# RWKV's triangular solve in blocks of 16 instead of 32, and every weight tile's low part on VectorE

## The chip, the cores and the metric

The kernel runs on one core of one Trainium2 chip, as one program. The metric is the device time of one launch in microseconds (us), the median of several runs. Five engines work side by side, each through its own instructions in order: TensorE (PE: matmuls, and PEld: its weight loads), VectorE (DVE), ScalarE (ACT), GpSimd (POOL) and SyncE (SP), which issues all DMAs of this kernel.

## The reference

One transformer-like block over 1024 positions of width 1024, in float32. A normalised input goes through one projection (`w_in`, 1024 x 3200), whose columns feed four mixers of 256 channels each: chunked attention, HGRN2, RWKV-7 and RG-LRU. Their outputs are joined, projected by `w_out`, normalised and added to the input; an MLP with squared ReLU (1024 to 4096 to 1024) follows.

```python
proj = (rms_norm(x, g_pre) @ w_in)
ya, yb, yc, yd = chunk_attention(..), hgrn2(..), rwkv7(..), rglru(..)
x = x + rms_norm(concatenate([ya, yb, yc, yd]) @ w_out, g_post)
x = x + rms_norm(square(relu(rms_norm(x, g_mlp) @ w1)) @ w2, g_mlp_post)
```

What matters here is RWKV-7's step, a recurrence over time with a state per head:

```python
sa = einsum('bhvk,bhk->bhv', state, -kk)
state = state * w + sa[..., None] * (kk * a) + v[..., None] * k
```

In chunks of 64 steps, the dependence of `sa` on earlier `sa` of the same chunk is a unit lower-triangular 64 x 64 system for each chunk and head. Its inverse is needed for 8 chunks and 4 heads, 32 systems, in each half of the sequence.

## The kernel before

The sequence is done in two halves of 512 positions (`hf` 0 and 1). For each half the four mixers run in the order of `ORDER`: RWKV, attention, LRU, HGRN in the first, RWKV, HGRN, attention, LRU in the second. Their instructions interleave: a planner orders each engine's instructions by a modelled time and by priorities (`PRIO`, `at(...)`), so the text's order is not the order on the engines. After that comes the output projection (`out_load`, `out_mm`, `residual`), and from about 715 us on the MLP, a Strassen-like scheme.

Matmuls are done in three passes for precision. A weight tile of 128 x 1024 is loaded raw (`wr`, L167), rounded by ScalarE to a high part (`wh`, L176), and the difference is the low part (`wl`, L178). With `hi` and `lo` of the activations, PE does `wh*hi`, `wl*hi` and `wh*lo` (L318 to L320, L345 to L347, L1023 to L1025). Raw, high and low tiles have two buffers each. `wparts` makes `wl` on GpSimd unless it is given an engine. Of 66 tiles 57 are made on GpSimd; the first tile of all and the eight of the second half's output projection on VectorE.

RWKV inverts each 64 x 64 system in `rwkv`, section `Ri`. The 64 x 64 matrix is cut into blocks of 32. `Ld` holds the diagonal blocks, `Lo` the block below. `Ld` goes through DRAM (`d1`) into `Lb`, with one system's rows in one partition: 64 blocks, each twice, since the two halves of the partitions do 16 columns of the inverse each. A loop of 31 steps on VectorE, two instructions each (L501 a product into `tmpx`, L503 a sum into `X`), is the substitution. `X` and its transpose go to DRAM (`d2`, L508, L509), and come back as matrices by partition in `XT` and `X11` (L516, L518). Two matmul stages of 64 small products (`p1`, L525; `p2`, L536) join the two 32-blocks to the 64 x 64 inverse in `XT`, which the recurrence over chunks (`Rk`) uses.

HGRN builds its attention in six levels: GpSimd makes `z` (L735, L736), ScalarE its exponential (L737), VectorE `z` and `zq` (L738, L747), PE `pz` (L750), VectorE writes it into `att` (L752). The names that the rows show besides: `pdg` (L264) spreads a column over rows at the start; `lx` (L931) is LRU's input; `q` (L698, L839) are HGRN's and attention's queries; `gg` and `th` (L719, L715) are HGRN's gate.

Of the kernel before, what the change touches and what calls it, by code (L numbers as in the profile page):

```python
# [20 lines left out]
F32 = mybir.dt.float32  # L21
# [6 lines left out]
MULT, ADD, SUB, MAX, MIN = ALU.mult, ALU.add, ALU.subtract, ALU.max, ALU.min  # L28
# [3 lines left out]
P = 128  # L32
# [8 lines left out]
CH = 64  # L41
# [47 lines left out]
def body(ctx: ExitStack, tc: tile.TileContext, A: dict, out: bass.AP, dbg=None, stop_after=None):  # L89
    nc = tc.nc  # L90
    V, S, G, T = nc.vector, nc.scalar, nc.gpsimd, nc.tensor

    const = ctx.enter_context(tc.tile_pool(name="const", bufs=1))
    dram = ctx.enter_context(tc.tile_pool(name="dram", bufs=1, space=DRAM))
# [6 lines left out]
    def at(*key):  # L101

        sec.close()
        n = PRIO.get("".join(map(str, key)), 0)
        if n:
            sec.enter_context(tc.high_priority(offset=n))

    def nm(base):
        uid[0] += 1
        return f"{base}_{uid[0]}"  # L110

    def bank(name, tag="pa"):
        return psp.tile([P, 512], F32, tag=tag, name=nm(name), bufs=PB[tag])
# [56 lines left out]
    def wload(src, eng=None):  # L170
        return wparts(wraw(src), eng)

    def wparts(raw, eng=None):
        wp = wpool[0]
        hi = wp.tile([P, 1024], F32R, tag="wh", name=nm("wh"))
        S.copy(hi[:], raw[:])  # L176
        lo = wp.tile([P, 1024], F32R, tag="wl", name=nm("wl"))
        (eng or G).tensor_tensor(lo[:], raw[:], hi[:].bitcast(F32), SUB)  # L178
        return hi, lo

    def split(eng_lo, hi, lo, src, scale=None):
# [15 lines left out]
    def u(name, dt=F32):  # L197
        return ma.tile([P, 512], dt, tag="ua", name=nm(name), bufs=NA)

    def u3(name, w, dt=F32):  # L200
        return ma.tile([P, 512 // w, w], dt, tag="ua", name=nm(name), bufs=NA)
# [13 lines left out]
    def w4(name, shape):  # L215
        return mx.tile(shape, F32, tag="w4", name=nm(name), bufs=2)
# [51 lines left out]
    def prep0():  # L268
        nc.sync.dma_start(vecs[:], A["vecs"])
        cols = W_LO, W_K  # L270
        hs, xs, ws = [], [], []
        for k in range(NK):
            xs.append(xload(0, k, lambda s, d, name: hp.tile(s, d, tag="hl", name=name, bufs=NLO)))
            if k < 2:
                ws.append(wraw(wsrc[cols[k]][0]))
        nc.sync.dma_start(ident[:], A["ident"])
        for k, h in enumerate(xs):
            hs.append(parts_in(0, k, h))
            if k < 2:
                early[cols[k]] = wparts(ws[k], (V, G)[k])  # L280
        stats(0)
        proj_pair(hs, *cols)
        spread(0)
        return hs
# [37 lines left out]
    def proj_fm(hs, col):  # L322

        if col in done:
            return done.pop(col)
        wh, wl = wload(wsrc[col][0])
        ps = bank("fm", "fm")
        for k in range(NK):
            mm_in(ps, wh, wl, hs, k)
        return ps  # L330
# [25 lines left out]
    def rwkv_shift(hf, ps, j, name):  # L356

        om = consts["om"]
        pc = u("pcs")
        V.tensor_tensor(pc[:], ps[:], rb_[hf][:], MULT)  # L360
        tmp = u("shtmp")
        S.activation(tmp[:], pc[:], AF.Identity, scale=om[:, j:j + 1])
        xs = u(name)
        V.scalar_tensor_tensor(xs[:, 1:TH], pc[:, 0:TH - 1], vec("mu", j), tmp[:, 1:TH], MULT, ADD)
        if hf == 0:
            V.tensor_copy(xs[:, 0:1], tmp[:, 0:1])
            V.tensor_copy(lastc[:, j:j + 1], pc[:, TH - 1:TH])
        else:
            V.scalar_tensor_tensor(xs[:, 0:1], lastc[:, j:j + 1], vec("mu", j), tmp[:, 0:1], MULT, ADD)
        return xs  # L370

    def rwkv(hf, hs):
# [13 lines left out]
        for j in range(2):  # L386
# [16 lines left out]
            k = rwkv_shift(hf, proj_fm(hs, W_K + j * P), 2 + j, "xk")  # L403
# [12 lines left out]
            for t in range(4):  # L416
                T.matmul(pss[:, 2 * t:2 * t + 2], sq[:, t * P:(t + 1) * P], consts["bones"][:],
                         start=True, stop=True)
# [15 lines left out]
            r = rwkv_shift(hf, proj_fm(hs, W_R + j * P), j, "xr")  # L434
# [30 lines left out]
        Ld, Lo = u3("Ld", 32), u3("Lo", 32)  # L465
# [8 lines left out]
        for b in range(4):  # L474
            r = slice(32 * b, 32 * b + 32)
            cc = 32 * (b % 2)
            S.copy(Ld[r].rearrange("q (p n) t -> q p n t", p=2), p4[r, :, :, cc:cc + 32])
        for c in range(2):
            r = slice(64 * c, 64 * c + 32)
            S.copy(Lo[r].rearrange("q (p n) t -> q p n t", p=2), p4[r, :, :, 32:64])  # L480
        at("Ri", hf)


        d1 = dram.tile([64, 32, 32], F32, tag="d1", name=nm("d1"), bufs=2)
        d2 = dram.tile([2, 64, 32, 32], F32, tag="d2", name=nm("d2"), bufs=2)
        d1v = d1[:].rearrange("(n b) s t -> b s n t", b=4)
        for b in range(4):
            nc.sync.dma_start(d1v[b], Ld[32 * b:32 * b + 32, :, :])
        Lb = w4("Lb", [P, 32, 32])
        for q in range(2):  # L490
            nc.sync.dma_start(Lb[64 * q:64 * q + 64], d1[:])
        X = u3("X", 16)
        G.memset(X[:], 0.0)
        for q in range(2):
            xq = X[64 * q:64 * q + 64, 16 * q:16 * q + 16, :].rearrange("p r c -> p (r c)")
            G.memset(xq[:, 0:256:17], 1.0)
        tmpx = u("tmpx")
        for jj in range(31):
            nr, ncl = 31 - jj, min(jj + 1, 16)
            tv = tmpx[:, 0:nr * ncl].rearrange("p (r c) -> p r c", c=ncl)  # L500
            V.tensor_tensor(tv, Lb[:, jj, jj + 1:32].unsqueeze(2).to_broadcast([P, nr, ncl]),  # L501
                            X[:, jj, 0:ncl].unsqueeze(1).to_broadcast([P, nr, ncl]), MULT)
            V.tensor_tensor(X[:, jj + 1:32, 0:ncl], X[:, jj + 1:32, 0:ncl], tv, ADD)  # L503
        XTt = u3("XTt", 32)
        V.tensor_copy(XTt[:], X[:].rearrange("p r c -> p c r"))
        for q in range(2):
            pq = slice(64 * q, 64 * q + 64)
            nc.sync.dma_start(d2[0, :, :, 16 * q:16 * q + 16], X[pq])  # L508
            nc.sync.dma_start(d2[1, :, 16 * q:16 * q + 16, :], XTt[pq])  # L509
        XT = w4("XT", [P, 16, CH])  # L510
        X11 = u3("X11", 32)
        d2v = d2[:].rearrange("k (n b) s t -> k b s n t", b=4)
        for b in range(4):
            r = slice(32 * b, 32 * b + 32)
            cc = 32 * (b % 2)
            nc.sync.dma_start(XT[r, :, cc:cc + 32], d2v[1, b])  # L516
            if b % 2 == 0:
                nc.sync.dma_start(X11[r, :, :], d2v[0, b])  # L518
            else:
                G.memset(XT[r, :, 0:32], 0.0)  # L520
        p1 = bank("p1")
        p13 = p1[:].rearrange("p (n c) -> p n c", c=32)
        for n in range(16):
            for c in range(2):
                T.matmul(p13[64 * c + 32:64 * c + 64, n, :], Lo[64 * c:64 * c + 32, n, :],  # L525
                         X11[64 * c:64 * c + 32, n, :], start=True, stop=True)
        T1 = u3("T1", 32)
        for c in range(2):
            r = slice(64 * c + 32, 64 * c + 64)
# [3 lines left out]
        for n in range(16):  # L533
            for c in range(2):
                r = slice(64 * c + 32, 64 * c + 64)
                T.matmul(p23[64 * c:64 * c + 32, n, :], T1[r, n, :], XT[r, n, 32:64], start=True, stop=True)  # L536
        for c in range(2):
            r = slice(64 * c, 64 * c + 32)
            S.copy(XT[r, :, 32:64], p23[r])

# [4 lines left out]
        for uu in range(2):  # L545
            for i in range(2):
# [28 lines left out]
                for o, M in ((pr, L2), (py, Ak)):  # L575
                    for h in range(4):
                        j, p = h // 2, h % 2
                        for cc in range(2):
                            T.matmul(o[half(cc), half(h)], M[p][j][half(cc)], vt[j][half(cc), ti, half(p)],
                                     start=(h == 0), stop=False, skip_group_check=True)  # L580
                for cc in range(2):
                    c = 2 * ti + cc
                    r = slice(64 * cc, 64 * cc + 64)
# [12 lines left out]
                    for h in range(4):  # L596
                        j, p = h // 2, h % 2
                        n = 8 * p + 2 * ti + j
                        T.matmul(pu[r, 64 * h:64 * h + 64], XT[r, n, :], Rs[r, 64 * h:64 * h + 64],
                                 start=False, stop=True, skip_group_check=True)  # L600
                    S.copy(Us[r, :], pu[r, :])
                    psS = bank("psS")
                    for h in range(4):
                        j, p = h // 2, h % 2
                        o = psS[64 * p:64 * p + 64, j * CH:(j + 1) * CH]
                        T.matmul(o, bk[r, 2 + j, 64 * p:64 * p + 64], vt[j][r, ti, 64 * p:64 * p + 64],
                                 start=(j == 0), stop=False, skip_group_check=True)
                    for h in range(4):
                        j, p = h // 2, h % 2
                        T.matmul(psS[half(p), half(j)], bk[r, j, half(p)], Us[r, half(h)],  # L610
                                 start=False, stop=True, skip_group_check=True)
                    Sn = Sbds[(8 * hf + c) % 2]
                    for p in range(2):
                        q = slice(64 * p, 64 * p + 64)
# [7 lines left out]
                for h in range(4):  # L622
                    j, p = h // 2, h % 2
                    for cc in range(2):
                        T.matmul(py[half(cc), half(h)], Ab[p][j][half(cc)], Us[half(cc), half(h)],
                                 start=False, stop=True, skip_group_check=True)
# [9 lines left out]
        for uu in range(2):  # L636
# [15 lines left out]
            for i in range(2):  # L652
                t = 2 * uu + i
                T.matmul(pg[:, 256 * i:256 * i + 256], lot[64:128, t * P:(t + 1) * P], lo2[64:128, :],
                         start=True, stop=True)
# [918 lines left out]
```

## Time and profile before

| | |
|---|---|
| median of 3 runs | 1427.42 us (1426.91 to 1429.3) |
| the profiled execution | 1431.72 us, of which 1429.9 us between its first and last instruction (the span) |
| PE busy | 1302.4 us (91%) |
| VectorE busy | 897.2 us (63%) |
| ScalarE busy | 659.2 us (46%) |
| GpSimd busy | 317.0 us (22%) |
| mean granted TensorE clock | 0.945 of full speed |

Busy time is the union of an engine's instructions. Matmuls are pipelined, and their ends are modelled, so that a busy PE is not PE at its peak. The granted clock has two levels, full (2.4 GHz) and half (1.2 GHz); a value between them is the mean over a stretch.

### The profile page before, as it was taken

The numbers are of one execution on the slowest core, as the hardware profiler recorded it, in microseconds if no ns is written. First come the engines' busy times: TensorE is split into PE (matmuls) and PEld (weight loads), VectorE is DVE, ScalarE is ACT, GpSimd is POOL, SyncE is SP. The second block draws the span as 40 slices with busy tenths as digits, with TensorE's granted clock in tenths as the row PEclk, the third lists the DMA queues.
The fourth block names the chain that finished last, engine by engine and source line by source line (L and its number), as shares of the span: only waits on it lengthen the run. The fifth ranks groups of instructions, "written<-read, shape, count | busy, mean of one in ns | idle before, by whom it ended". The sixth has DMA issues, their size and how long they took to land. (4 is left out here: it accounts for less than half of the span.)

```text
span 1429.9 us, 20091 instructions
## 1 busy us (share of the span) xinstructions
PE 1302.4 (91%) x7528; PEld 1026.6 (72%) x7528; DVE 897.2 (63%) x1528; ACT 659.2 (46%) x1157; POOL 317.0 (22%) x246
## 2 busy tenths in 40 slices
PE   5887899888987899998889789999999999999997
PEld 4676677656767678765667667888887788888886
DVE  5647535675648346766475898888774644545884
ACT  5622635554252235565465744545543533433441
POOL 2242223344234214312512312222220000000000
PEclk9998999998889689999999999999999999999999
DMA  8223111311122201123653179777663976555661
GB/s 275 99 82 86 60 46 59 122 58 50 38 74 74 57 16 60 52 67 109 225 192 118 60 255 310 262 268 260 226 238 137 358 256 239 191 191 191 229 271 59
DMA packets 104513, 215.35 MB, mean 151 GB/s; under 512 B 28896, under 2 KB 31840, under 8 KB 104416
## 3 DMA queue, kind: packets, MB, share of 16 engines
q1 hardware_dynamic: 104416, 214.07, 43.9%
q8 instruction: 59, 0.97, 0.3%
q14 instruction: 38, 0.31, 0.1%
HBM read 157.94 MB, written 56.10 MB: 150 GB/s over the span
## 5 line engine op out<-in xcount | busy, mean ns | idle before, releaser
L178 POOL TENSOR_TENSOR wl<-wr,wh 128x1024 fp32r<-128x1024 f32 x57 | 138.9, 2438 | 334.5 <-ACT wh L176 289.1
L1359 PE MATMUL q<-b,a 128*128 128x512 f32 x448 | 175.7, 393 | 2.4 <-ACT b L1343 2.4
L1360 PE MATMUL q<-b,a 128*128 128x512 f32 x448 | 176.6, 394 | 1.3 <-DVE b L1344 1.3
L1361 PE MATMUL q<-b,a 128*128 128x512 f32 x448 | 176.4, 394 | 0.0
L318 PE MATMUL fm<-hh,wh 128*128 128x512 f32 x304 | 133.4, 440 | 20.3 <-ACT wh L176 7.7
L319 PE MATMUL fm<-hh,wl 128*128 128x512 f32 x304 | 132.3, 436 | 3.8 <-POOL wl L178 3.3
L320 PE MATMUL fm<-hl,wh 128*128 128x512 f32 x304 | 132.0, 436 | 0.0
L176 ACT CAST wh<-wr 128x1024 fp32r<-128x1024 f32 x66 | 68.8, 1043 | 85.0 <-issue 36.0
L1359 PEld LDWEIGHTS q<-b,a 128*128 128x128 f32 x448 | 84.4, 189 | 21.4 <-ACT b L1343 2.8
L1360 PEld LDWEIGHTS q<-b,a 128*128 128x128 f32 x448 | 84.9, 189 | 20.5 <-DVE b L1344 1.7
L1361 PEld LDWEIGHTS q<-b,a 128*128 128x128 f32 x448 | 84.8, 189 | 19.0
L318 PEld LDWEIGHTS fm<-hh,wh 128*128 128x128 f32 x304 | 62.0, 204 | 38.9 <-issue 9.4
L319 PEld LDWEIGHTS fm<-hh,wl 128*128 128x128 f32 x304 | 62.3, 205 | 20.2 <-POOL wl L178 4.3
L1344 DVE TENSOR_TENSOR b<-wb,b 128x1024 fp32r<-128x1024 f32 x32 | 39.2, 1224 | 59.3 <-ACT b L1343 59.0
L320 PEld LDWEIGHTS fm<-hl,wh 128*128 128x128 f32 x304 | 62.0, 204 | 16.6 <-issue 4.3
L1344 DVE TENSOR_TENSOR a<-ha,a 128x1024 fp32r<-128x1024 f32 x56 | 68.2, 1218 | 6.3 <-ACT a L1343 6.1
L1094 ACT CAST s<-w 128x512 fp32r<-128x512 f32 x64 | 39.1, 618 | 68.5 <-DVE w L1175 20.9
L1343 ACT CAST b<-wb 128x1024 fp32r<-128x1024 f32 x32 | 33.5, 1048 | 78.4 <-PE q L1360 63.3
L1095 POOL TENSOR_TENSOR w<-w,w 128x512 fp32r<-128x512 f32 x32 | 48.7, 1531 | 85.8 <-ACT w L1094 85.8
L1344 DVE TENSOR_TENSOR b<-wt,b 128x1024 fp32r<-128x1024 f32 x24 | 29.4, 1225 | 55.9 <-ACT b L1343 55.9
L345 PE MATMUL tm<-wh,hh 128*128 128x256 f32 x192 | 57.4, 299 | 7.5 <-DVE q L698 5.0
L1343 ACT CAST a<-ha 128x1024 fp32r<-128x1024 f32 x56 | 58.6, 1046 | 8.4 <-DMA ha<-hx 8.4
(1082 smaller groups left out, 3240.4 us busy)
## 6 DMA issues: line engine op xcount, KB each, us to landing
ha<-hx SPq DMA_DIRECT2D x56, 512.0 KB, 4.5
wr<-in_win_dram SPq DMA_DIRECT2D x50, 512.0 KB, 3.6
w<-in_w_dram SPq DMA_DIRECT2D x36, 512.0 KB, 5.0
wb<-in_w_dram SPq DMA_DIRECT2D x32, 512.0 KB, 7.3
wt<-tx SPq DMA_DIRECT2D x32, 512.0 KB, 3.2
w2s<-in_w_dram SPq DMA_DIRECT2D x48, 256.0 KB, 4.1
tx<-w2s SPq DMA_DIRECT2D x48, 256.0 KB, 2.4
hx<-h SPq DMA_DIRECT2D x48, 256.0 KB, 3.4
```

The lines of the kernel that those rows point to most:

```text
L176: S.copy(hi[:], raw[:])
L178: (eng or G).tensor_tensor(lo[:], raw[:], hi[:].bitcast(F32), SUB)
L318: T.matmul(ps[:], wh[:, ks], hi[:], start=(k == 0), stop=False, skip_group_check=True)
L319: T.matmul(ps[:], wl[:, ks], hi[:], start=False, stop=False, skip_group_check=True)
L320: T.matmul(ps[:], wh[:, ks], lo[:], start=False, stop=(k == NK - 1), skip_group_check=True)
L345: T.matmul(o, hi[:, tsl], wh[:, cs], start=(k == 0 and t % 2 == 0), stop=False, skip_group_check=True)
L1095: eng.tensor_tensor(t[:, 1, :], src, t[:, 0, :].bitcast(F32), SUB)
L1343: S.copy(h_, r[:])
L1344: V.tensor_tensor(l_, r[:], h_.bitcast(F32), SUB)
L1359: T.matmul(o, ah[:, i, tsl], bh[:, i, :], start=start, stop=False, skip_group_check=True)
L1360: T.matmul(o, ah[:, i, tsl], bl[:, i, :], start=False, stop=False, skip_group_check=True)
L1361: T.matmul(o, al[:, i, tsl], bh[:, i, :], start=False, stop=stop, skip_group_check=True)
```

## The change

Two things change. In `wparts` every low part is made on VectorE, whatever engine is named. In `rwkv` the diagonal blocks are 16 x 16: 128 of them, one in each partition, in a loop of 15 steps. Four blocks of 32 rows are then put together from two blocks of 16 by two more matmul stages (`p0`, then `p0t` and `p0n`), with copies by ScalarE and two sums on VectorE, before `p1` and `p2` follow as they were.

```diff
-        (eng or G).tensor_tensor(lo[:], raw[:], hi[:].bitcast(F32), SUB)
+        V.tensor_tensor(lo[:], raw[:], hi[:].bitcast(F32), SUB)
...
-        d1 = dram.tile([64, 32, 32], F32, tag="d1", name=nm("d1"), bufs=2)
-        d2 = dram.tile([2, 64, 32, 32], F32, tag="d2", name=nm("d2"), bufs=2)
-        for b in range(4):
-            nc.sync.dma_start(d1v[b], Ld[32 * b:32 * b + 32, :, :])
-        Lb = w4("Lb", [P, 32, 32])
-        for q in range(2):
-            nc.sync.dma_start(Lb[64 * q:64 * q + 64], d1[:])
...
-        for jj in range(31):
-            nr, ncl = 31 - jj, min(jj + 1, 16)
...
-        for q in range(2):
-            nc.sync.dma_start(d2[0, :, :, 16 * q:16 * q + 16], X[pq])
-            nc.sync.dma_start(d2[1, :, 16 * q:16 * q + 16, :], XTt[pq])
-        for b in range(4):
-            nc.sync.dma_start(XT[r, :, cc:cc + 32], d2v[1, b])
-            if b % 2 == 0:
-                nc.sync.dma_start(X11[r, :, :], d2v[0, b])
+        d1 = dram.tile([P, 16, 16], F32, tag="d1", name=nm("d1"), bufs=2)
+        d2 = dram.tile([2, P, 16, 16], F32, tag="d2", name=nm("d2"), bufs=2)
+        for b in range(8):
+            c = 16 * (b % 2)
+            nc.sync.dma_start(d1v[b], Ld[16 * b:16 * b + 16, :, c:c + 16])
+        nc.sync.dma_start(Lb, d1[:])
...
+        XT = w4("XT", [P, 16, CH])
+        X11, AB = u3("X11", 32), w4("AB", [P, 16, 48])
+        G.memset(XT[:], 0.0)
+        G.memset(X11[:], 0.0)
+        G.memset(AB[:, :, 16:32], 0.0)
+        for jj in range(15):
+            nr, ncl = 15 - jj, jj + 1
+            V.tensor_tensor(tv, Lb[:, jj, jj + 1:16]..., X[:, jj, 0:ncl]..., MULT)
+            V.tensor_tensor(X[:, jj + 1:16, 0:ncl], X[:, jj + 1:16, 0:ncl], tv, ADD)
+        V.tensor_copy(XTt, X.rearrange("p r c -> p c r"))
+        nc.sync.dma_start(d2[0], X)
+        nc.sync.dma_start(d2[1], XTt)
         for b in range(4):
+            nc.sync.dma_start(AB[r, :, 0:16], d2v[0, 2 * b])
+            nc.sync.dma_start(AB[r, :, 32:48], d2v[1, 2 * b + 1])
+            nc.sync.dma_start(XT[r, :, c:c + 16], d2v[1, 2 * b])
+            nc.sync.dma_start(XT[r2, :, c + 16:c + 32], d2v[1, 2 * b + 1])
             if b % 2 == 0:
+                nc.sync.dma_start(X11[r, :, 0:16], d2v[0, 2 * b])
+                nc.sync.dma_start(X11[r2, :, 16:32], d2v[0, 2 * b + 1])
+        for n in range(16):
+            for r in quarters:
+                T.matmul(p03[r, n, :], Ld[r, n, 16:32], AB[r, n, 0:16], start=True, stop=True)
+        for r in quarters:
+            S.copy(T0[r], p03[r])
+        for n in range(16):
+            for b, r in enumerate(quarters):
+                T.matmul(p0t[r, n, :], T0[r, n, :], AB[r, n, 32:48], start=True, stop=True)
+                if b % 2 == 0:
+                    T.matmul(p0n[32 * b:32 * b + 32, n, :], AB[r, n, 16:48], T0[r, n, :], start=True, stop=True)
+        for b, r in enumerate(quarters):
+            S.copy(XT[r, :, c + 16:c + 32], p0t[r])
+            if b % 2 == 0:
+                V.tensor_tensor(X11[r, :, 0:16], p0n[r], X11[r, :, 0:16], ADD)
```

## Rows read from the trace of the kernel before

**Rows 1.** The page, its first line: span and instructions.

```profile
span 1429.9 us, 20091 instructions
```

**Rows 2.** Stages: length; busy of PE, PEld, DVE, ACT, POOL; clock; DMA share; GB/s.

```profile
0.00:715.00 715.00, 618.57 (x4585) 474.34 (x4586) 416.31 (x930) 326.73 (x624) 224.30 (x186) 0.91 0.27 85
715.00:1430.00 715.00, 683.80 (x2945) 552.29 (x2943) 480.89 (x599) 332.45 (x535) 92.67 (x60) 0.98 0.61 216
```

**Rows 3.** Waits of PE, 0 to 715 us: total, times, longest (us).

```profile
PE pz L750 <- DVE zq L747: 20.1, 9, 9.9
PE fm L318 <- DVE lx L931: 5.2, 1, 5.2
PE tm L345 <- DVE q L698: 5.0, 1, 5.0
PE rb L265 <- DVE pdg L264: 4.7, 3, 2.2
...
PE fm L318 <- ACT th L715: 3.5, 2, 2.8
...
PE fm L319 <- POOL wl L178: 3.3, 3, 1.6
...
PE tm L345 <- DVE q L839: 2.5, 1, 2.5
...
PE fm L319 <- DVE wl L178: 0.5, 1, 0.5
```

**Rows 4.** Timeline of VectorE, second half's substitution: start, us, instruction, idle before.

```profile
427.62 1.79 DVE L501 TENSOR_TENSOR tmpx<-Lb,X 128x31 f32<-128x31 f32 x1 [0.91 <-DMA Lb<-d]
...
433.98 2.44 DVE L503 TENSOR_TENSOR X<-X,tmpx 128x192 f32<-128x192 f32 x1
...
460.02 0.59 DVE L505 COPY XTt<-X 128x512 f32<-128x512 f32 x1
460.52 0.89 DVE L719 SCALAR_TENSOR_TENSOR gg<-th 128x128 f32<-128x128 f32 x4
...
465.47 2.92 DVE L747 TENSOR_TENSOR zq<-z,q 64x256 f32<-64x256 f32 x2
```

**Rows 5.** Timeline of GpSimd at the same time.

```profile
433.61 2.60 POOL L178 TENSOR_TENSOR wl<-wr,wh 128x1024 fp32r<-128x1024 f32 x1 [4.26 <-ACT wh L176]
```

**Rows 6.** Timeline of VectorE, two other stretches.

```profile
24.72 0.48 DVE L264 TENSOR_SCALAR pdg<-ident,rs 128x128 f32<-128x128 f32 x2
25.59 4.62 DVE L264 TENSOR_SCALAR pdg<-ident,rs 128x128 f32<-128x128 f32 x2 [0.39 <-PE rb L265]
...
353.18 4.00 DVE L747 TENSOR_TENSOR zq<-z,q 64x256 f32<-64x256 f32 x2
```

**Rows 7.** Groups by line: busy us, mean ns | idle before, releasers.

```profile
L178 POOL TENSOR_TENSOR wl<-wr,wh 128x1024 fp32r<-128x1024 f32 x57 | 138.9, 2438 | 334.5 <-ACT wh L176 289.1 <-issue 43.7 <-DVE sg L398 1.1
...
L1024 PE MATMUL po<-wl,mh 128*128 128x512 f32 x128 | 53.7, 420 | 6.5 <-DVE wl L178 5.2 <-POOL wl L178 1.3
...
L178 DVE TENSOR_TENSOR wl<-wr,wh 128x1024 fp32r<-128x1024 f32 x9 | 12.0, 1341 | 12.8 <-ACT wh L176 12.7
```

**Rows 8.** Groups by form, VectorE, 100 to 135 us: small steps of the substitution.

```profile
L501 DVE TENSOR_TENSOR tmpx<-Lb,X 128x64 f32<-128x64 f32 x1 | 0.2, 225 | 0.0
...
L501 DVE TENSOR_TENSOR tmpx<-Lb,X 128x16 f32<-128x16 f32 x1 | 0.2, 176 | 0.0
```

**Rows 9.** Busy time around the two substitutions' ends, columns as in group 2.

```profile
128.00:140.00 12.00, 6.83 (x30) 5.68 (x28) 8.29 (x18) 3.65 (x5) 4.73 (x2) 0.72 0.45 88
454.00:474.00 20.00, 7.23 (x26) 5.66 (x25) 13.12 (x38) 3.28 (x6) 8.23 (x9) 0.66 0.46 99
```

**Rows 10.** Busy time of `p1` (L525), then `p2` (L536), in two stretches: PE, PEld, clock.

```profile
140.00:160.00 20.00, 1.44 (x64) 1.22 (x64) 1.00 0.30 74
...
480.00:495.00 15.00, 2.22 (x64) 1.96 (x64) 0.73 0.12 37
```

**Rows 11.** DMA issues on SP that load `XT` (L516): ns min/median/max.

```profile
L516 SPq DMA_DIRECT2D XT<-d x8: 302/478/489, 139.0 to 468.1; - x8
```

More of the change, by code (lines that the diff above doesn't have):

```diff
@@ L481, in rwkv @@
         at("Ri", hf)
-        d1 = dram.tile([64, 32, 32], F32, tag="d1", name=nm("d1"), bufs=2)
-        d2 = dram.tile([2, 64, 32, 32], F32, tag="d2", name=nm("d2"), bufs=2)
-        d1v = d1[:].rearrange("(n b) s t -> b s n t", b=4)
-        for b in range(4):
-            nc.sync.dma_start(d1v[b], Ld[32 * b:32 * b + 32, :, :])
-        Lb = w4("Lb", [P, 32, 32])
-        for q in range(2):
-            nc.sync.dma_start(Lb[64 * q:64 * q + 64], d1[:])
-        X = u3("X", 16)
-        G.memset(X[:], 0.0)
@@ L494, in rwkv @@
-        for q in range(2):
-            xq = X[64 * q:64 * q + 64, 16 * q:16 * q + 16, :].rearrange("p r c -> p (r c)")
-            G.memset(xq[:, 0:256:17], 1.0)
-        tmpx = u("tmpx")
-        for jj in range(31):
-            nr, ncl = 31 - jj, min(jj + 1, 16)
[L500 to L507, printed above, removed]
-            nc.sync.dma_start(d2[0, :, :, 16 * q:16 * q + 16], X[pq])
-            nc.sync.dma_start(d2[1, :, 16 * q:16 * q + 16, :], XTt[pq])
-        XT = w4("XT", [P, 16, CH])
-        X11 = u3("X11", 32)
-        d2v = d2[:].rearrange("k (n b) s t -> k b s n t", b=4)
-        for b in range(4):
-            r = slice(32 * b, 32 * b + 32)
-            cc = 32 * (b % 2)
-            nc.sync.dma_start(XT[r, :, cc:cc + 32], d2v[1, b])
-            if b % 2 == 0:
-                nc.sync.dma_start(X11[r, :, :], d2v[0, b])
-            else:
-                G.memset(XT[r, :, 0:32], 0.0)
+        d1 = dram.tile([P, 16, 16], F32, tag="d1", name=nm("d1"), bufs=2)
@@ new lines, in rwkv @@
+        d2 = dram.tile([2, P, 16, 16], F32, tag="d2", name=nm("d2"), bufs=2)
+        d1v = d1[:].rearrange("(n b) s t -> b s n t", b=8)
+        d2v = d2[:].rearrange("k (n b) s t -> k b s n t", b=8)
+        for b in range(8):
+            c = 16 * (b % 2)
+            nc.sync.dma_start(d1v[b], Ld[16 * b:16 * b + 16, :, c:c + 16])
+        Lw = u3("Lb", 16)
+        Lb, T0 = Lw[:, 0:16, :], Lw[:, 16:32, :]
+        nc.sync.dma_start(Lb, d1[:])
+        X2 = u3("X", 16)
+        X, XTt = X2[:, 0:16, :], X2[:, 16:32, :]
@@ new lines, in rwkv @@
+        G.memset(X, 0.0)
+        G.memset(X.rearrange("p r c -> p (r c)")[:, 0:256:17], 1.0)
+        XT = w4("XT", [P, 16, CH])
[3 more added lines that the diff above has]
+        G.memset(AB[:, :, 16:32], 0.0)
+        tmpx = T0.rearrange("p r c -> p (r c)")
+        for jj in range(15):
+            nr, ncl = 15 - jj, jj + 1
+            tv = tmpx[:, 0:nr * ncl].rearrange("p (r c) -> p r c", c=ncl)
+            V.tensor_tensor(tv, Lb[:, jj, jj + 1:16].unsqueeze(2).to_broadcast([P, nr, ncl]),
+                            X[:, jj, 0:ncl].unsqueeze(1).to_broadcast([P, nr, ncl]), MULT)
+            V.tensor_tensor(X[:, jj + 1:16, 0:ncl], X[:, jj + 1:16, 0:ncl], tv, ADD)
@@ new lines, in rwkv @@
+        V.tensor_copy(XTt, X.rearrange("p r c -> p c r"))
+        nc.sync.dma_start(d2[0], X)
+        nc.sync.dma_start(d2[1], XTt)
+        for b in range(4):
+            r, r2 = slice(32 * b, 32 * b + 16), slice(32 * b + 16, 32 * b + 32)
+            c = 32 * (b % 2)
+            nc.sync.dma_start(AB[r, :, 0:16], d2v[0, 2 * b])
+            nc.sync.dma_start(AB[r, :, 32:48], d2v[1, 2 * b + 1])
+            nc.sync.dma_start(XT[r, :, c:c + 16], d2v[1, 2 * b])
+            nc.sync.dma_start(XT[r2, :, c + 16:c + 32], d2v[1, 2 * b + 1])
+            if b % 2 == 0:
+                nc.sync.dma_start(X11[r, :, 0:16], d2v[0, 2 * b])
+                nc.sync.dma_start(X11[r2, :, 16:32], d2v[0, 2 * b + 1])
@@ new lines, in rwkv @@
+        quarters = [slice(32 * b, 32 * b + 16) for b in range(4)]
+        p0 = bank("p0")
+        p03 = p0[:, 0:256].rearrange("p (n c) -> p n c", c=16)
+        for n in range(16):
[3 more added lines that the diff above has]
+            S.copy(T0[r], p03[r])
+        pt_ = bank("p0")
+        p0t = pt_[:, 0:256].rearrange("p (n c) -> p n c", c=16)
+        p0n = pt_[:, 256:512].rearrange("p (n c) -> p n c", c=16)
@@ new lines, in rwkv @@
+        for n in range(16):
[4 more added lines that the diff above has]
+        for b, r in enumerate(quarters):
+            c = 32 * (b % 2)
+            S.copy(XT[r, :, c + 16:c + 32], p0t[r])
+            if b % 2 == 0:
+                r = slice(32 * b, 32 * b + 32)
+                V.tensor_tensor(X11[r, :, 0:16], p0n[r], X11[r, :, 0:16], ADD)
```

## The prediction

> **What bounds the kernel now.** The span is 1429.9 us of a profiled execution of 1431.72 us [rows 1]. First read busy time by stage [rows 2]: in the second half PE is busy 684 of 715 us at a granted clock of 0.98, and nothing of the change runs there but a little of the output projection. In the first half PE is busy 619 of 715 us at 0.91, so some 96 us are holes and more is lost to the clock. Whatever the change gives or takes is in these holes, in the clock behind them, or in PE work added. VectorE is busy 416 us there (58%), GpSimd 224.
>
> Next read what ended PE's holes [rows 3]. VectorE did, mostly: 18 groups, from 20.1 us (`zq`) down to 0.5 us (`wl`), sum to 63.6 us, 8.9% of the stage. GpSimd's own `wl` ended only 3.3 us of the projections' holes. So GpSimd's 57 tiles seem well hidden.
>
> Now read what VectorE does in the substitution [rows 4]. It starts at 427.62 us and its transpose at 460.02, 32.4 us later; the first half's took 31.3 us. Right behind it come four `gg` that ScalarE's `th` waits for, and `zq`, which PE waits for. One step takes 2.44 us, though it has no more elements than neighbours of 0.4 us: at 433.61 GpSimd begins a `wl` of 2.60 us, and the step ends when that ends [rows 5]. Elsewhere two `pdg` take 0.48 us, the next two 4.62; two `zq` take 4.00 us [rows 6]. This is one pattern. Instruction by instruction, 41 VectorE instructions of the stage that ran beside an L178 were longer by 64.2 us together than the shortest of their line and shape, 1.6 us each. GpSimd's tiles hold VectorE up, and the waits charge it to VectorE.
>
> **The low parts on VectorE.** Removed: 57 x 2438 ns = 138.9 us of GpSimd and with them the 64.2 us of holds. Added to VectorE: 57 tiles. Nine are there already, at a mean of 1341 ns [rows 7]: 76.4 us. VectorE's sum is thus nearly unchanged (416 - 64 + 76 = 428), and the gain is in where the delays fall. Nine holds stand just ahead of a PE hole: two `pdg` (2.0, 1.8), a substitution step ahead of `q` L839 (2.1), the instruction ahead of `q` L698 (2.2), two ahead of transposes (2.2, 2.0), three `zq` (2.0, 2.2, 2.1), each at the lesser of hold and hole. Without the last, which lies in the substitution's hole below, eight make 16.5 us. The new tiles also stand ahead of such instructions. A tile on VectorE takes about half as long as on GpSimd, so an instruction that comes at any time meets one half as often and waits half as long for its end: a quarter, 4.1 us. Net 12.4 us. As bounds: all 16.5 at one end; at the other nothing, if VectorE's 76.4 us fall as badly as the 64.2 did.
>
> The Trainium skill says in "GPSIMD Engine Reference", section 1 (Specifications), that GpSimd shares its SBUF interfaces with VectorE and contends with VectorE instructions that have two SBUF inputs. By that rule HGRN's two-input instructions on GpSimd, which stay, can hold the new tiles on VectorE too; no row here shows such a tile by itself. By the rule the sum would be no other, since the mean price of the nine has such meetings in it.
>
> The second price is a wait in the queue. A `wl` needs its `wh`, which needs a free buffer, which PE frees. On GpSimd this wait was 289.1 us for ScalarE [rows 7], at no cost, for little stood behind it. On VectorE everything stands behind it: LRU, `zq`, the state updates, softmax. The nine tiles there waited 12.8 us, 1.4 each. 57 x 1.4 = 81 us of VectorE's 299 idle us, of which 8.9% reach PE as its delays do now: 7.2 us. The other bound is what PE itself waited for tiles on VectorE: 5.2 + 0.5 us for nine [rows 3, 7], 0.63 each, or 36 us for 57. The 5.2 us are one event among them, in the output projection, where VectorE waited long for one `wh`. I take 7.2, since eight of nine cost PE nearly nothing, and keep 36 for the range.
>
> PE's own waits for GpSimd tiles halve with the tile's time: 3.3 gives 1.6 us.
>
> **The substitution.** A new step has 15 to 64 elements, 176 to 225 ns [rows 8]. With some 40 ns between instructions, 30 of them take about 7.4 us, against 32.4 and 31.3. VectorE is free 24 us earlier in each half. The holes behind it: 9.9 us for `zq` and 2.8 for `th` in the second half, 5.2 for `lx` in the first [rows 3], 17.9 us in all. After them the granted clock is 0.66 and 0.72 [rows 9]; the busy time there at the missing share, 7.23 x 0.34 + 6.83 x 0.28 = 4.4 us, comes back if the holes close. What is late next: `gg` ran at 460.52, right behind the loop [rows 4]; with the loop done by 436 it runs when its own inputs come, and GpSimd's `z` and its exponential, which lead to `zq`, move ahead with it, so the hole can close wholly. Bounds: 22.3 us at one end, 0 if the next chain (ScalarE, GpSimd, VectorE) is as late.
>
> The new matmul stages: 64 + 96 products a half. 64 of the old ones took 1.44 us at full clock, 2.22 at a mixed one [rows 10]; 160 cost 3.6 to 5.6. One half at each price: 9.2 us of PE time, which nothing hides, for PE is the bound. If they fit into holes they cost 0.
>
> Eight short copies on ScalarE a half, two sums on VectorE and three fills on GpSimd are hidden: none of these engines is over 60% busy, and RWKV's chain has room, as follows. DMA issues on SP rise from 16 to 31 a half. At 478 ns for a load of this kind [rows 11], the 20 loads that now end the chain take 9.6 us against 2.9, and the two stages with copies some 8 us more. This takes some 15 of the 24 us back, so that RWKV's inverse is ready about 9 us earlier, and no hole of PE in rows 3 waits for it. Weight loads stand behind these issues on SP; two buffers cover about two tiles of PE work. Without that cover it costs up to 6.7 us a half.
>
> The Trainium skill, "DMA: Bandwidth & Descriptors", Specifications, asks for at least 512 B a piece for full rate. The pieces shrink from 128 to 64 B here. By that rule the loads would land later, and this speaks against the change; no row here times such a load by itself.
>
> **Sum.** Gains 17.9 + 4.4 + 12.4 + 1.6 = 36.3; costs 9.2 + 7.2 = 16.4; net 19.9 us. 1431.7 - 19.9 = 1411.8 for the profiled execution, which lies 4.3 us above the median of the runs: 1407.5, say 1407 us.
>
> **Rivals.**
>
> *The queue wait decides (slower).* Place: VectorE's queue, a `wl` at its head that waits for `wh`. The gains less PE's new work are 27.1 us; over 57 tiles the change turns slower when a tile delays PE by more than 0.48 us. At the measured 0.63 it costs 36 us: 1427.4 + 9 = 1436. For it: the hole of 5.2 us [rows 7]. Against it: that is one tile of nine, in a stage where the residual's and the transposes' work crowd VectorE.
>
> *The holes move (no change).* The planner lays out every engine anew; HGRN's chain from GpSimd over ScalarE to VectorE takes the substitution's place as what is late, and 22.3 us of gain are not there: about 1429, within 1424.6 to 1430.3. For it: other `zq` waits where no substitution ran (20.1 less 9.9 in eight). Against it: VectorE is then idle where it was full.
>
> *More comes back.* RWKV's inverse comes early enough to fill later holes, PE's new products fall into holes (9.2 us) and half of the remaining `zq` and `pdg` waits go with their clock: some 19 us more, 1388.
>
> *Pieces of 64 B.* If the loads of the chain landed 10 us later than now, the inverse would come as late as before; RWKV then gains nothing, but the holes behind the substitution close all the same: 1407 to 1410. It is not told apart by the time and has no chance of its own.
>
> **How the numbers follow.** The sum as forecast 0.50, from 1396 to 1421 by one hole of 10 us either way with its clock; the queue wait 0.25; no change 0.14; more 0.11. The range is 1387 to 1439: the rivals' times, with a little for the unknown order above 1436. A measurement tells 0.2% (2.9 us) from no change. Faster takes the first and the last case and a bit of the third (0.50 x 0.95 + 0.11 + 0.04), 0.63; same 0.12; slower 0.25.
>
> **What would show it.** Right: VectorE's instructions in the mixers close to the shortest of their shape; L178 on VectorE 66 times near 1.2 to 1.3 us; the substitution 7 to 8 us; no hole of 10 us before `zq` in the second half and none before `lx`; the mixers' clock above 0.91; GpSimd near 85 us in that stage. Wrong: VectorE's idle time before L178 of more than 150 us, and PE waits for `wl` or for VectorE work just behind a waiting `wl`, above 30 us; or PE's holes in the mixers still near 96 us with ScalarE or GpSimd at their ends. Were the order on PE wholly different from before, the holes named here could not be matched one to one, and the sum would be right or wrong only as a whole.

## The result, and the profile after

The changed kernel takes 1372.51 us (median of four, 1367.63 to 1384.74), against 1428.21 us (1426.91 to 1429.3) for the kernel before beside it: a ratio of 0.962, with a 95% interval of 0.9583 to 0.9657. That is 54 us faster by the ratio. The forecast was 20 us, and the time lies 14 us below its range. One execution of all the runs below (1764.67 us, another order) fell into a slower state of the chip and is left out.

The first two lines of the page of the kernel after, whose profiled execution took 1376.2 us:

```profile
span 1374.3 us, 21361 instructions
PE 1289.0 (94%) x8168; PEld 1016.8 (74%) x8168; DVE 881.9 (64%) x1525; ACT 661.8 (48%) x1171; POOL 181.0 (13%) x189
```

Its stages, in the columns of [rows 2]. The first ends 56 us ahead of the MLP's first product, as 715 us did before (55):

```profile
0.00:660.00 660.00, 614.51 (x5268) 471.87 (x5269) 401.65 (x936) 334.38 (x646) 88.86 (x129) 0.95 0.28 90
660.00:1374.00 714.00, 674.50 (x2902) 544.95 (x2900) 480.21 (x590) 327.44 (x525) 92.14 (x61) 0.98 0.63 216
```

The second stage is as long as it was. The first is 55 us shorter: PE's holes fall from 96 to 45 us and the clock rises from 0.91 to 0.95. PE's waits up to 660 us, to set against [rows 3]:

```profile
PE fm L318 <- ACT wh L176: 8.3, 3, 6.7
PE pz L776 <- DVE zq L773: 5.0, 8, 1.1
PE pcp L583 <- ACT Lo L480: 4.7, 2, 4.2
PE rb L265 <- DVE pdg L264: 2.7, 3, 2.0
...
PE fm L319 <- DVE wl L178: 0.9, 2, 0.5
```

The wait for `zq` falls from 20.1 to 5.0 us, and its longest from 9.9 to 1.1; `lx` and `q` are gone. The tiles that VectorE now makes cost the projections 0.9 us. Groups by line, for the tiles, the substitution and the new products (busy us, mean ns | idle before, releasers), to set against [rows 7, 8]:

```profile
L178 DVE TENSOR_TENSOR wl<-wr,wh 128x1024 fp32r<-128x1024 f32 x66 | 83.4, 1265 | 45.3 <-ACT wh L176 45.0
L507 DVE TENSOR_TENSOR Lb<-Lb,X 128x15 f32<-128x15 f32 (+7 forms) x30 | 6.1, 204 | 0.8
L509 DVE TENSOR_TENSOR X<-X,Lb 128x15 f32<-128x15 f32 (+7 forms) x30 | 6.2, 207 | 0.9
L529 PE MATMUL p<-AB,Ld 16*16 16x16 f32 x256 | 3.6, 176 | 1.3 <-DMA AB<-d 1.3
L537 PE MATMUL p<-AB,Lb 16*16 16x16 f32 x256 | 6.3, 188 | 1.6 <-ACT Lb L531 1.0 <-issue 0.3
L539 PE MATMUL p<-Lb,AB 16*32 16x16 f32 x128 | 6.1, 207 | 1.0 <-issue 1.0
```

The tiles, at 1265 ns, are what was forecast, and so is the loop's work, 6.2 us a half. From its first to its last step it takes 8.7 us in the first half and 11.3 in the second, since low parts and other work of VectorE now run between its steps. VectorE's timeline at the end of the second loop, to set against [rows 4]:

```profile
407.07 0.17 DVE L509 TENSOR_TENSOR X<-X,Lb 128x15 f32<-128x15 f32 x1
407.28 0.39 DVE L510 COPY X<-X 128x256 f32<-128x256 f32 x1
407.58 1.22 DVE L178 TENSOR_TENSOR wl<-wr,wh 128x1024 fp32r<-128x1024 f32 x1
413.61 1.22 DVE L178 TENSOR_TENSOR wl<-wr,wh 128x1024 fp32r<-128x1024 f32 x1 [4.81 <-ACT wh L176]
422.89 0.49 DVE L745 SCALAR_TENSOR_TENSOR gg<-th 128x128 f32<-128x128 f32 x2 [8.05 <-ACT th L742]
```

The loop no longer stands in front of `gg`: that runs 15.6 us after it, and VectorE waits for its input.

Four numbers split the time up to the MLP's first product, for every kernel of this study. Holes are the time in which PE is idle. The trace's clock records give PE's busy time at 1.2 GHz; half of it is what the clock cost. PE's busy time less that half is its work at full clock. Holes, work and half of the third column add up to the first. The numbers are those of the one profiled execution of each kernel, which can lie a few us off the median.

| us | MLP's first product | PE's holes | PE busy at 1.2 GHz | PE's work at full clock |
|---|---|---|---|---|
| before | 769.9 | 101.2 | 109.7 | 613.8 |
| after | 715.9 | 59.0 | 71.6 | 621.1 |

So 42.2 us of holes and 19.0 of clock came back, 7.3 us of PE work were added, and what follows the MLP's first product, up to VectorE's last instruction, gave 1.7 us.

VectorE's holds can be seen in whole groups of one shape. Before, two groups by shape:

```profile
L747 DVE TENSOR_TENSOR zq<-z,q 64x256 f32<-64x256 f32 x48 | 30.9, 644 | 1.5 <-ACT z L741 1.1
L264 DVE TENSOR_SCALAR pdg<-ident,rs 128x128 f32<-128x128 f32 x8 | 6.2, 800 | 3.3 <-PE rb L265 3.2
```

After:

```profile
L773 DVE TENSOR_TENSOR zq<-z,q 64x256 f32<-64x256 f32 x48 | 22.3, 464 | 0.4
L264 DVE TENSOR_SCALAR pdg<-ident,rs 128x128 f32<-128x128 f32 x8 | 2.1, 285 | 0.9 <-PE rb L265 0.7
```

The same work, 8.6 and 4.1 us shorter. "Held" below is that difference taken for each instruction: its length less the shortest of its line and shape, where it ran beside an instruction of GpSimd. Beside L178 it was 64.6 us before the MLP (41 instructions), and is 0 after.

### The profile page after: what moved, and what is told of

It reads as the page before. It is cut to its first block, busy times and chain, and to the rows that moved or that the text cites. A ratio compares the mean times of both kernels' runs of the same rounds, so it can differ in the third digit from the quotient of the medians.

```text
span 1374.3 us, 21361 instructions
## 1 busy us (share of the span) xinstructions
PE 1289.0 (94%) x8168; PEld 1016.8 (74%) x8168; DVE 881.9 (64%) x1525; ACT 661.8 (48%) x1171; POOL 181.0 (13%) x189
## 5 line engine op out<-in xcount | busy, mean ns | idle before, releaser
L178 DVE TENSOR_TENSOR wl<-wr,wh 128x1024 fp32r<-128x1024 f32 x66 | 83.4, 1265 | 45.3 <-ACT wh L176 45.0
L1386 PEld LDWEIGHTS q<-b,a 128*128 128x128 f32 x448 | 84.9, 189 | 20.5 <-DVE b L1370 1.7
L1120 ACT CAST s<-w 128x512 fp32r<-128x512 f32 x64 | 39.1, 618 | 66.1 <-DVE w L1193 19.5
L1050 PE MATMUL po<-wl,mh 128*128 128x512 f32 x128 | 52.0, 408 | 9.9 <-DVE wl L178 9.9
```

Of the source, the lines that this page charges most:

```text
L178: V.tensor_tensor(lo[:], raw[:], hi[:].bitcast(F32), SUB)
L1050: T.matmul(pss[t][:], hi[:, tsl], wl[:, cs], start=False, stop=False)
L1386: T.matmul(o, ah[:, i, tsl], bl[:, i, :], start=False, stop=False, skip_group_check=True)
```

## The experiments

Two parts were changed at once, so each was run alone. The theory: GpSimd's low parts hold VectorE, each held microsecond delays the end wherever it falls in the mixers, and the blocks give nothing. The rivals: the low part itself was late on GpSimd (2.4 us instead of 1.3), or the blocks close the holes, as the prediction said.

**The low parts alone** (the kernel before with this line):

```diff
-        (eng or G).tensor_tensor(lo[:], raw[:], hi[:].bitcast(F32), SUB)
+        V.tensor_tensor(lo[:], raw[:], hi[:].bitcast(F32), SUB)
```

> The kernel before with one line changed: all low parts on VectorE, the solve still in blocks of 32. Theory 'holds' (the 57 GpSimd tiles held VectorE up, and most of the gain is that these holds and the half clock behind them are gone): about 1385 us, PE holes before the MLP near 70 us instead of 101, half clock near 95 us instead of 133. Theory 'solve' (the gain is VectorE set free 24 us earlier in each half): about 1415 us, with the holes before the LRU input (5 us) and before the second half's first HGRN level (10 us) still there.

Measured: 1353.28 us, ratio 0.9476 (0.9432 to 0.9521). One line gives 75 us, 19 more than the whole change. The theory had the direction and not the size: 1385 us, with 95 us of half clock (idle time counted in), where 31 are left.

**The blocks alone** (the changed kernel with that line as before):

> The changed kernel with the low parts back on GpSimd, so only the solve in blocks of 16 is left of the change. Theory 'holds': about 1415 us (the terms of the prediction for the solve alone: 17.9 + 4.4 - 9.2 = 13 us), with some 30 VectorE instructions still held beside a GpSimd tile. Theory 'solve': about 1385 us. If the two parts only pay together, both single parts stay above 1400 us.

Measured: 1430.65 us, ratio 1.0007 (0.9971 to 1.0044): nothing, where even the theory of holds had put the blocks at 1415. Beside L178, 39 VectorE instructions are still held here, for some 59 us. PE's waits there up to 715 us, and behind 715 us:

```profile
PE pz L776 <- DVE zq L773: 11.2, 8, 2.2
...
PE tm L345 <- DVE q L724: 5.9, 2, 5.0
...
PE p L537 <- issue: 3.7, 2, 2.3
PE p L529 <- DMA AB<-d: 3.5, 2, 2.4
...
PE h L1255 <- ACT yo L1090: 10.9, 1, 10.9
```

The hole of 9.9 us for `zq` is closed (the longest is 2.2), the one for `lx` too, and `th` falls from 2.8 to 0.6 us, as forecast. But `p0` and `p0t` bring 7.2 us of waits, and one of 10.9 us stands just ahead of the MLP. Holes fall by 7.9 us in all, PE's work rises by 8.0, and the clock gives 0.6.

**The hold put back.** To tell the hold from the tile's lateness, the changed kernel got useless work on GpSimd behind each of the 57 low parts; the low parts stay on VectorE. Two inputs, one input, or none:

```diff
+        if eng is not V:
+            G.tensor_tensor(raw[:], h, h, SUB)       # first: two inputs read
+            G.tensor_copy(raw[:], h)                 # second: one input read
+            G.memset(raw[:], 0.0)                    # third: no input, done twice
```

> The changed kernel, and behind each of 57 low parts on VectorE one GpSimd instruction of the old shape that nobody needs: 128 x 1024, two inputs read from the high part (subtracted from itself), written into the raw tile that is no longer needed. VectorE has the same work as in the changed kernel. Theory 'holds': VectorE instructions are held again for some 40 to 80 us in total, and the time rises to 1400 to 1425 us. Rival 'latency' (the gain is that a low part is ready after 1.2 us instead of 2.4, and VectorE's turn-taking with GpSimd costs nothing): stays within 1365 to 1385 us.

> The full change with a useless GpSimd copy of the high tile (128 x 1024, one input read instead of two) behind each of the 57 low parts, where the two-input dummy cost 55 us (1427.5) and the two fills 13 (1385.2). Theory 'only two-input work on GpSimd holds VectorE': near the fills, 1372 to 1388, with VectorE held by under 12 us beside it. Rival 'whatever reads SBUF on GpSimd holds VectorE': 1400 or above, held by 30 us or more.

> As the run before, but the useless GpSimd work is two fills of the raw tile with zeros (no input read, about the same 2.1 us of GpSimd and the same later release of the raw tile). If it is the reading of two inputs that holds VectorE up, no VectorE instruction is lengthened beside a fill and the time stays within 1365 to 1390 us. If it is GpSimd's queue being busy (HGRN's levels behind it) or the raw tile's later release, the time rises as much as with the two-input work, to 1400 us or more.

Measured: 1427.47 us, ratio 0.9988 (0.9964 to 1.0012), with two inputs; 1394.41, 0.9748 (0.9714 to 0.9783), with one; 1385.17, 0.9705 (0.9644 to 0.9765), with the fills. The groups of this work on GpSimd, two inputs:

```profile
L181 POOL TENSOR_TENSOR wr<-wh 128x1024 f32<-128x1024 f32 x57 | 114.8, 2015 | 316.7 <-DVE wl L178 257.5 <-issue 39.6 <-DMA wr<-in_win_dram 7.4
```

One input:

```profile
L180 POOL COPY wr<-wh 128x1024 f32<-128x1024 f32 x57 | 66.7, 1171 | 328.9 <-DVE wl L178 273.7 <-issue 35.7 <-DVE stat L915 12.9
```

None:

```profile
L181 POOL MEMSET wr<- 128x1024 f32 x114 | 109.3, 960 | 298.0 <-DVE wl L178 271.0 <-issue 24.1
```

| behind each low part, on GpSimd | GpSimd busy with it | VectorE held beside it | slower than the change |
|---|---|---|---|
| two inputs | 114.8 us | 50.5 us (39 instructions) | 53 us |
| one input | 66.7 us | 19.5 us (30) | 18 us |
| fills | 109.3 us | 6.2 us (14) | 12 us |

(The last column is the difference of the ratios times 1428 us.) Useless work that nothing waits for but the buffer takes the whole gain back, so the tile's lateness falls as the cause. GpSimd is as busy with fills as with the two inputs, so it isn't its busy time either: the loss follows what VectorE is held, at roughly 1 us for each held microsecond (up to 2 with the fills, where both numbers are small). The copies came out between the two sides that had been put down; they hold too, but for less. A copy is also shorter (1171 ns against 2015), so these two runs do not tell the number of inputs from the length. And VectorE instructions that met other work of GpSimd besides can be counted either way: with them, the fills' holds come to some 10 us.

The Trainium skill, "SBUF — State Buffer", Who interferes with whom, says that a VectorE instruction with two SBUF inputs contends with GpSimd instructions that read SBUF, and not with those that only write it. The runs agree, nearly: fills of 109.3 us held VectorE by 6.2 us.

**The joining stages taken out** (the 160 small products, their copies and sums; nothing else):

```diff
-        p0 = bank("p0")
...
-                V.tensor_tensor(X11[r, :, 0:16], p0n[r], X11[r, :, 0:16], ADD)
```

> The changed kernel without the two matmul stages that join the blocks of 16 (160 small products a half, their eight copies by ScalarE and two sums on VectorE are left out, so the lower left 16 x 16 part of each 32-block of the inverse stays zero). Everything else stays, the loop of 15 steps, its 31 DMA issues and the low parts on VectorE. Theory 'the joining stages': of the 19 us by which the full change is slower than the low parts alone, about 9 are PE work and the rest is the half clock around the stages; both go, 1372.5 - 19 = 1353, and at most 1358, with less than 45 us of half clock before the MLP (82 in the changed kernel, 31 with the low parts alone). Rival 'the DMAs or the new order': the issues of 64-byte pieces, or only another plan, cost it; then only the 8.6 us of PE work go, and it stays at 1362 to 1367 or above.

Measured: 1361.12 us, ratio 0.9519 (0.9449 to 0.959), between the theory and the rival. Against the full change PE's work falls by 5.5 us and the clock gives 10.0, which is the joining stages' part; 8 us remain to the low parts alone, though the two intervals overlap. Half clock is left for 58 us (in the expectation's count), where less than 45 was forecast.

**A joining stage put in** behind the loop of 31 steps:

```diff
+                T.matmul(p03[r, n, :], Ld[r, n, 16:32], XT[r, n, c:c + 16], start=True, stop=True)
...
+            S.activation(T0[r], p03[r], AF.Identity, scale=0.0)
...
+                T.matmul(p0t[r, n, :], T0[r, n, :], XT[r, n, c:c + 16], start=True, stop=True)
...
+                    T.matmul(p0n[32 * b:32 * b + 32, n, :], XT[r, n, 0:32], T0[r, n, :], start=True, stop=True)
...
+                V.tensor_tensor(X11[r, :, 0:16], p0n[r], X11[r, :, 0:16], ADD)
```

> The low parts alone (blocks of 32, loop of 31 steps, the old DMAs) with joining stages added that add nothing to the result: the same 160 small products a half between the loads of XT and p1, the eight copies by ScalarE (the first four with a factor of 0, so that what is written and added behind them is zero) and the two sums on VectorE. Theory 'the joining stages cost PE work and the half clock around them': taken out of the full change they gave 11.4 us back; added here they cost as much, 1353.3 + 11.4 = 1365, within 1360 to 1370, and PE's work before the MLP rises from 612.5 to some 619 to 621 us. Rival 'only in the order of the full change': they fall into holes here, at most 1357. Rival 'they cost all that the blocks cost': 1372.

Measured: 1393.26 us, ratio 0.9731 (0.9691 to 0.9772): 36 us lost, three times what was expected and more than either rival allowed.

**The short loop alone:**

```diff
-        for jj in range(31):
+        for jj in range(16, 31):
```

> The low parts alone with the loop of the substitution cut to its last 15 steps (steps 0 to 15 are left out, so the inverses are incomplete); products, sums and DMAs behind it stay. It frees VectorE some 13 us earlier in each half and adds nothing. The prediction's claim, that a shorter loop closes holes of PE, would give 10 us or more: 1343 or below. Theory 'without the holds the loop is hidden': no change, 1349 to 1358. Rival 'the shorter loop lets RWKV's small products crowd together, at half clock', as the kernel without the joining stages suggests, which is still 8 us behind the low parts alone: 1358 to 1363, with a stretch of half clock of 20 us near 345 us.

Measured: 1361.14 us, ratio 0.9511 (0.945 to 0.9572). A gain of 10 us is excluded. The time lies 3 us above the range of 'hidden' and within that of 'crowd together', but its interval overlaps that of the low parts alone, so that no loss is shown, and the stretch of half clock at 346 us lasted 10.2 us and not 20.

**Another order.** One number of `PRIO` changed, in the low parts alone and in the full change:

```diff
-"Rk11": 85
+"Rk11": 60
```

> The low parts alone with one number of the planner's table changed (Rk11 from 85 to 60), which alters the order on PE and on the other engines and no work. A control: if the order by itself is worth about as much as the 19 us between the low parts alone (1353.3) and the full change (1372.5), this run lies more than 10 us from 1353. If the joining stages set that difference, it lies within 8 us, 1345 to 1361.

> The full change with the same number changed (Rk11 from 85 to 60). If the joining stages set the 19 us, it lies within 8 us of 1372.5, 1364 to 1381, and still 10 us or more behind the low parts alone in the same order. If the order by itself is worth as much, it can fall to the 1353 of the low parts alone, or rise above 1385.

Measured: 1351.81 us, 0.9475 (0.94 to 0.955), and 1367.16 us, 0.9585 (0.9519 to 0.9651): 0 and 5 us from their pairs. This one change of order is worth less than the differences that are read here as effects of the joining stages; how far another order would go, it does not show.

**The same rule in the MLP.** With the low parts alone, VectorE's instructions are still longer than their shortest by 60.7 us over the whole program, mostly beside the residual's sums and the MLP's splits on GpSimd. They go to VectorE too:

```diff
-                (V if n else G).tensor_tensor(y[:], y[:], xt[:], ADD)
+                V.tensor_tensor(y[:], y[:], xt[:], ADD)
...
-            w = [parts(r0[:, i * 512:(i + 1) * 512], "w11", G) for i in range(2)]
+            w = [parts(r0[:, i * 512:(i + 1) * 512], "w11", V) for i in range(2)]
...
-            mm1(d, parts(A11, "s3", G), Bt[3], True, True)
+            mm1(d, parts(A11, "s3", V), Bt[3], True, True)
...
-            bsplit(1, k, b11[k], V if k % 2 else G)
+            bsplit(1, k, b11[k], V)
```

> The low parts alone (blocks of 32 as before), and besides GpSimd's remaining two-input work in the output stage and the MLP is put on VectorE: one of the residual's sums, the parts of w11 and s3, and the splits of the MLP's tiles. Theory 'holds cost where PE waits': VectorE is held by about 26 us at L1095 and 7 us at L1052 there, but PE has only some 18 us of holes in that stage, so it gains 0 to 12 us on the 1353.3 of the low parts alone: 1341 to 1353. Rival 'a hold costs its own length wherever it falls': it gains the whole of some 40 us, 1313. Rival 'VectorE becomes late': its 36 us of new work stand in front of what PE waits for, 1360 or above.

Measured: 1342.77 us, ratio 0.9405 (0.9344 to 0.9465), the fastest of all. Its interval overlaps that of the low parts alone, but each of its executions (1338.97 to 1347.73) was shorter than each of theirs (1350.96 and above). That excess falls by 47 us, the time from the MLP's first product to VectorE's last instruction from 658.7 to 648.0. Where PE is nearly always busy a held microsecond costs about 0.2 us, net of the work that VectorE took over.

The same split of the time as above, for all kernels:

| us | MLP's first product | PE's holes | PE busy at 1.2 GHz | PE's work at full clock |
|---|---|---|---|---|
| low parts alone | 687.2 | 60.3 | 28.9 | 612.5 |
| blocks alone | 769.4 | 93.3 | 108.6 | 621.8 |
| after, two-input work | 769.6 | 91.3 | 114.2 | 621.1 |
| after, one-input work | 736.2 | 72.4 | 80.0 | 623.8 |
| after, fills | 718.9 | 66.4 | 56.9 | 624.0 |
| after, no joining | 701.2 | 59.8 | 51.7 | 615.6 |
| low parts, joining added | 732.7 | 68.3 | 82.4 | 623.2 |
| low parts, short loop | 696.9 | 57.3 | 49.5 | 614.9 |
| low parts, other order | 688.2 | 61.1 | 27.2 | 613.6 |
| after, other order | 711.9 | 54.9 | 64.9 | 624.6 |
| low parts, MLP splits too | 684.6 | 59.3 | 26.8 | 612.0 |

Against before, the low parts alone give 40.9 us of holes and 40.4 of clock: as much by the clock as by the holes (the two profiled executions lie 81 us apart). And the blocks, on top of them, cost 8.6 us of work and 21.3 of clock. Three windows of the kernel after show where, in the columns of [rows 2]; in the first and the last the joining stages run. At 120.6 and 427.8 us the clock is at 1.2 GHz for 10.2 us each; without the joining stages there is none near either, and half of the two is about the 10.0 us of clock that the stages cost:

```profile
118.00:134.00 16.00, 14.47 (x399) 9.77 (x399) 8.60 (x12) 9.63 (x20) 0.95 (x1) 0.68 0.21 69
345.00:372.00 27.00, 25.00 (x162) 17.58 (x163) 10.10 (x20) 3.13 (x7) 3.10 (x4) 0.62 0.11 39
425.00:440.00 15.00, 12.50 (x379) 9.83 (x365) 8.54 (x18) 8.00 (x18) 5.35 (x7) 0.66 0.22 73
```

With the low parts alone, the window that has the products of the second of these (RWKV's `plt`, HGRN's `pin` and `po`, among projections):

```profile
328.00:350.00 22.00, 21.15 (x192) 15.86 (x190) 15.73 (x33) 5.24 (x10) 5.18 (x9) 1.00 0.14 49
```

PE is nearly as busy in the former (25.00 of 27 us) as in the latter (21.15 of 22), but at 0.62 instead of 1.00. The half clock began there, at 349.3 us, within a run of small products (`pnb`, `pdt`, `pke`, `plt`, `pin`) without a projection between them from 345.4 to 352.2 us; with the low parts alone this run is shorter, 335.8 to 338.6 us.

Loop and joining, all with the low parts on VectorE, as ratios to before:

| | no joining | joining |
|---|---|---|
| loop of 31 steps | 0.9476 | 0.9731 |
| short loop | 0.9511 (old DMAs), 0.9519 (new DMAs) | 0.962 |

The joining stages cost 36 us behind the long loop and 14 behind the short one. Only where they are there is the short loop worth something, 16 us (the two kernels compared differ in their DMAs besides), and that does not pay for them. In the case of the 36 us (43 between the profiled executions), holes cost 8.0, PE's work 10.7 and the clock 26.8; RWKV's first product with the inverse (`pu`) begins at 162.7 us instead of 148.2. That this lateness is what lowers the clock is not shown.

## Why the prediction was wrong

The sign, the tiles' price, the loop's work and the clock above 0.91 came as forecast. By parts, the prediction gave the low parts 6.8 us (12.4 + 1.6 - 7.2) and the blocks 13.1 (17.9 + 4.4 - 9.2); run alone they gave 75 and nothing. GpSimd was busy 88.9 us in the first stage (85 forecast). By kinds, the sum reads:

| us gained | predicted | measured |
|---|---|---|
| PE's holes (17.9 + 12.4 + 1.6 - 7.2) | 24.7 | 42.2 |
| clock | 4.4 | 19.0 |
| PE's work | -9.2 | -7.3 |
| behind the MLP's start | 0 | 1.7 |

**The holds: the step that failed.** The prediction had found the 64.2 us of holds, and then charged only eight of them, "just ahead of a PE hole", 16.5 us less a quarter. Alone, the low parts gave 75 us, and two-input work put back took 53. The rule that a hold counts only if PE waits for that very instruction is wrong here, by a factor of four to six. The likely reading is that the waits name the last link of a chain, and that a hold anywhere in it is inherited; which way each hold takes to PE was not traced. No clock was charged to the holds at all; it was half of what the low parts alone gave before the MLP.

**The substitution.** The 17.9 us of holes did close, with the blocks alone: `zq`, `lx`. The 22.3 us were still not gained, for the sum of holes fell by 7.9 us only. This part went as the rival "the holes move" put it: next late were the waits at `p0`, a chain of ScalarE, and tail work of the output stage. And much of those holes were holds themselves: without the low parts on GpSimd the two instructions of the loop of 31 steps take 19.8 us of VectorE's time a half; before it was 29.0.

**The new products.** 9.2 us of PE work were forecast, and 7.3 more were measured in all. That they are near is luck. A float32 product of these stages is two instructions of the profile: `p1` and `p2` have 32 products each a half, and not 64 as said above, and [rows 10] count 64 instructions. The prediction priced 160 new products as if they were 160 of these; they are 320 a half (640 in the three groups above), which at its own prices is 18 us. The smaller products then took half the time each, and kept PE busy for 10.3 us in all:

```profile
152.42 1.19 PE L525 MATMUL p<-X,Lo 32*32 32x32 f32 x62
118.29 1.17 PE L529 MATMUL p<-AB,Ld 16*16 16x16 f32 x122
```

(The first line is of the kernel before, the second of the one after.) What the term lacked is their clock: the windows above are at 0.66 and 0.68, and of the 14.6 us that the stages cost in the changed kernel 10.0 are clock.

**The small pieces.** PE waited 1.3 us for `AB`'s loads in all, 3.5 with the blocks alone. The loads did not land later than the old ones, which were four times as large; loads, KB each, median us from issue to landing, before and after:

```profile
XT<-d SPq DMA_DIRECT2D x8, 64.0 KB, 2.5
```

```profile
XT<-d SPq DMA_DIRECT2D x16, 16.0 KB, 2.2
AB<-d SPq DMA_DIRECT2D x16, 16.0 KB, 2.2
```

**The queue wait.** VectorE idled 45.3 us before its 66 tiles, where 81 were forecast for 57, and PE waited 0.9 us for them in the projections; 7.2 was too much. There is one more wait for a tile, in the output projection, of 5.2 us before [rows 7] and more after:

```profile
PE po L1050 <- DVE wl L178: 9.9, 1, 9.9
```

The prediction took the 5.2 us as VectorE's wait for a `wh`, and drew the slower rival's price from it. VectorE's timeline before shows something else: VectorE did the residual's work without a pause up to that tile, whose `wh` had been ready for 8 us.

```profile
718.95 1.42 DVE L1051 SCALAR_TENSOR_TENSOR yo<-yo,ors,gpost 128x512 f32<-128x512 f32 x2
...
720.88 2.46 DVE L1051 SCALAR_TENSOR_TENSOR yo<-yo,ors,gpost 128x512 f32<-128x512 f32 x2
...
729.76 3.42 DVE L178 TENSOR_TENSOR wl<-wr,wh 128x1024 fp32r<-128x1024 f32 x2
```

And GpSimd's:

```profile
720.44 1.69 POOL L1052 TENSOR_TENSOR yo<-yo,xres 128x512 f32<-128x512 f32 x1 [13.52 <-DVE yo L1051]
...
729.31 1.65 POOL L1052 TENSOR_TENSOR yo<-yo,xres 128x512 f32<-128x512 f32 x1 [1.29 <-DVE yo L1051]
```

Two scalings take 1.42 us alone and 2.46 beside GpSimd's sum, three times over, and the tile behind them is held too (3.42 us for two): 4 us of the 5.2. In the kernel after, GpSimd's splits for the MLP run beside the residual as well, and two scalings take up to 3.47 us. In the run with the MLP's splits moved GpSimd does neither; every two scalings take 1.41 us, VectorE does the four sums besides, and the wait is

```profile
PE po L1024 <- DVE wl L178: 3.4, 1, 3.4
```

against 5.9 us with the low parts alone. So most of the evidence for the slower rival was holds, and none of it a wait for `wh`.

**GpSimd's own tiles** ended 3.3 us of PE's waits in the projections, and VectorE's end 0.9 (0.5 before): 2.9 us less instead of 1.6.

**What stays open.** Why the low parts alone, but with a shorter loop or without joining stages, have 20 us more of PE's busy time at half clock than with the long loop. That the order of the small products around 345 us does it is argued from two windows only. And why the blocks cost 19 us without the holds and nothing with them: with them the added work is met by 7.9 us fewer holes and no loss of clock, but what makes the difference was not tried.

## What to carry to other kernels

Compare each instruction with the shortest of its own shape: time lost to another engine is not in any list of waits. Where chains run over several engines, charge such a hold with about its full length, even if PE does not wait for that instruction (here 75 us for 65 held, half of it through PE's clock); where PE is nearly always busy, with a fifth. Count a stage's price in the profile's own instructions, not in calls of the program. When a change has two parts, one may pay for the other: here one line alone was worth 75 us, and the rest on top of it cost 19.

## What the runs showed of the hardware

A GpSimd instruction with two SBUF inputs of 128 x 1024 delays VectorE instructions that start beside it to its end or a little beyond (0.4 us became 2.4). A copy of the same size, itself 1171 ns long against 2015, held each instruction that it held for 0.65 us on average, against 1.3, and fills hardly held any. And after a run of small products PE's clock was at 1.2 GHz for 20.5 us, though PE was busy for 25.0 of the 27.0 us around it.
